# A second attention with doubled query and key columns, whole transposes, alternating value products and head norms from one square

## The chip, the cores and the metric

The kernel runs on one core of a Trainium2 chip. The metric is the device time of one execution in microseconds (us), the median of the runs shown. A profiled execution gives the span of its instructions and a trace. In its rows PE is TensorE (matrix products and transposes), PEld its weight loads, DVE is VectorE, ACT is ScalarE, POOL is GpSimd and SP the engine that issues most loads.

## The reference, cut to what matters

Two transformer blocks of two layers each follow each other on 256 tokens of width 1024. The change lies in the second layer of the second block (an attention that also reads 256 context tokens) and in two helpers that earlier layers use too.

```python
qkv = h_lat @ w_qkv
q = rmsnorm(qkv[..., :Q_DIM].reshape(B, S, N_Q_HEADS, HEAD_DIM), q_g)      # 16 heads of 64
k = rmsnorm(qkv[..., Q_DIM:Q_DIM + KV_DIM].reshape(B, S, N_KV_HEADS, HEAD_DIM), k_g)   # 4 heads
q = apply_rope(q, cos, sin)
k = apply_rope(k, cos, sin)
kv_c = h_ctx @ w_qkv[:, Q_DIM:]
k_all = jnp.concatenate([k_c, k], axis=1)     # 256 context + 256 own tokens
v_all = jnp.concatenate([v_c, v], axis=1)
s = jnp.einsum('bqhgd,bkhd->bhgqk', q_blk, k_all)
p = jax.nn.softmax(s, axis=-1)
o = jnp.einsum('bhgqk,bkhd->bqhgd', p, v_all)
```

## The kernel before, in words

All weights come from DRAM as a fixed list of pieces. Each piece lands in a buffer (`raw`, or a lent `page`), ScalarE rounds it to a high part `H` (L309) and VectorE forms the low part `L`, the rest (L310); a product takes three matrix products, high by high, low by high and high by low (`mm3`, L149 to L151). Between the weights stand pieces of the modulation matrices, which VectorE multiplies by a scalar and accumulates (L353). When eight of those are summed, `ada_piece` reduces them over the 128 rows, in most cases with transposes and eight ScalarE activations that sum along the row (L364) and whose elementwise output, `adump`, nobody reads.

The order on each engine is decided by a scheduler when the program is built, from the order of the code and priorities; an engine then takes its instructions strictly in that order. Tiles come from rotating pools: PSUM has three banks `mm`, four `acc` and one `tr`; 512-column work tiles are called `q1` to `q4`, two buffers each.

Block 1 (two layers) norms its query and key heads with `head_rstd`: one ScalarE square of 64 columns with a sum for each head (L617), then a power on GpSimd. `head_rope` rotates: two products with tables of cosines and sines (L635, L636), one difference and one sum (L639, L640).

`attention2` is the second attention. Four projections give keys and values of 256 context and 256 own tokens (`kpost`), two more give the queries of eight heads each (`qpost`). Scores need query and key with the 64 head columns on the partitions, twice: the query's high part in one half of the 128 rows and its low part in the other, the key's high part in both halves, so that one product gives both. `twice` does that from rows of 64 columns a head: for each of four heads one transpose into rows 0 to 63 (L1519) and one product with the identity into rows 64 to 127 (L1520, two instructions on the engine). `kH` and `kL` are the key's two parts; `kL` holds two of the four key heads in rows 0 to 63 and two in rows 64 to 127. Work that `later` defers runs some projection parts later.

Then a loop over 16 heads, in which step i does `S(i)`, the scores and their softmax, `T(i-1)`, the transposes of the probabilities, and `O(i-2)`, the product with the values:

- `S`: for each of two token tiles a product with `kH` on 128 rows (L1576) and one with `kL` on 64 rows (L1577), VectorE's maximum (L1579), ScalarE's exponent with its sum (L1583), VectorE's reciprocal and scaling (L1584, L1585).
- `T`: eight 128x128 transposes (L1594) and two ScalarE copies to `pT` (L1597).
- `O`: four products of a 128x64 value tile (L1608, eight instructions on the engine); even heads write rows 0 to 63 and odd heads rows 64 to 127 of one PSUM bank, which is read after the odd head (L1612, L1613).

Behind it come the output projection and the expert layer.

Of the kernel before, what the change touches and what calls it, by code (L numbers as in the profile page):

```python
# [24 lines left out]
P = 128  # L25
# [58 lines left out]
class Kern:  # L84
# [256 lines left out]
    def ada_piece(s, raw, m, j, q):  # L341
# [12 lines left out]
        if q == 7:  # L354
            for v in vecs:
                if (m, j) not in ((0, 0), (0, 1)) and (m < 3 or j == 1):
                    u = s.st([P, 8], tag="acol8", bufs=4)
                    for h in range(2):
# [3 lines left out]
                        for i in range(4):  # L362
                            o = s.st([P, P], tag="adump", bufs=1)
                            nc.scalar.activation(o, t[:, i * P:(i + 1) * P], AF.Copy, accum_out=u[:, 4 * h + i:4 * h + i + 1])  # L364
# [26 lines left out]
    def far_row(s, col, new=None):  # L391
        """as row, through DRAM"""
# [200 lines left out]
    def kt(H, Lo, t):  # L593
        """the k tiles of token tile t"""
# [16 lines left out]
    def head_rstd(s, src, nh):  # L611
        """src [P, nh*64] -> 1 / rms of each head"""
        nc = s.nc
        ss = s.st([P, 8], tag="hss", bufs=4)
        for h in range(nh):
            o = s.st([P, P], tag="adump", bufs=1)
            nc.scalar.activation(o[:, 0:64], src[:, h * 64:(h + 1) * 64], AF.Square, scale=0.125, accum_out=ss[:, h:h + 1])  # L617
# [11 lines left out]
    def head_rope(s, qn, nh, CG, SG, w, dst, psum=False):  # L629
# [7 lines left out]
        hv = lambda t: t[:, 0:n].rearrange("p (a b w) -> p a b w", b=2, w=w)  # L637
        c, sn, d = hv(qc), hv(qs), hv(dst)
# [3 lines left out]
    def block1(s, l):  # L642
# [80 lines left out]
        # output projections of the two attentions, gated  # L723
# [33 lines left out]
        # mlp  # L757
# [93 lines left out]
    def proj(s, ps, X, key, kk, n, post=None, first=True, last=True, tmajor=False, late=False):  # L851
        """n half pieces of kk k-tiles against the token tiles; late: the low parts last"""
# [127 lines left out]
    def lat_rows(s):  # L980
        """the rows that the pool layer needs for x, made ahead"""
# [45 lines left out]
    def pre0(s, X):  # L1027
        """pool mixer, then the router's logits and the rows that the experts gather"""
# [26 lines left out]
    def slots0(s, t0, before=(), slot0=None):  # L1055
        """where the expert inputs and weights of two token tiles go in the slots"""
# [39 lines left out]
    def ctx_steps(s):  # L1096
        """the pool layer's work on the context, in steps, each after the modulation vectors that it needs"""
# [37 lines left out]
    def ctx_step(s, last=False):  # L1135
        """the next step if its vectors are there; all that is left if last"""
# [57 lines left out]
    def ranks(s, M16, n, before=()):  # L1194
        """M16 [P, 2, n] 0/1 -> [P, 3, n]: how many came before, and the counts"""
# [17 lines left out]
    def dense_rest(s, l, fl, hD, ovg, Xs, rows, bank, hT, mo, wt):  # L1213
        """tokens that found no slot: every expert over all tokens, weighed by ovg"""
# [89 lines left out]
    def router(s, Ac, Sc):  # L1304
        """the router's weights with the norm's gain in them, and its bias with the shift"""
# [182 lines left out]
    def attention2(s):  # L1488
# [111 lines left out]
        def O(h):  # L1600
            b = (h % 2) * 64
            if h % 2 == 0:
                ops[h // 2] = s.mm()
# [257 lines left out]
```

## Time and profile before

| | |
|---|---|
| device time, median of 3 runs | 1524.44 us (1520.88 to 1526.36) |
| span of the profiled execution | 1517.5 us |
| median less that span | 6.9 us |
| TensorE busy | 1386.3 us, 91% of the span |
| VectorE busy | 1175.7 us, 77% |
| ScalarE busy | 936.0 us, 62% |
| mean granted clock of TensorE | 0.951 |

Which of the runs was profiled isn't marked, so its own time is taken as the span and the 6.9 us by which the median lies above it. A share over the whole span mixes stages with different limits; the rows below are cut by stage. TensorE's products are pipelined, so that one product's duration is longer than the distance to the start of the next; paces are read from starts. A granted clock of 1.00 is 2.4 GHz and 0.50 is 1.2 GHz.

### The profile page before, as it was taken

The numbers are of one execution on the slowest core, as the hardware profiler recorded it, in microseconds if no ns is written. First come the engines' busy times: TensorE is split into PE (matmuls) and PEld (weight loads), VectorE is DVE, ScalarE is ACT, GpSimd is POOL, SyncE is SP. The second block draws the span as 40 slices with busy tenths as digits, with TensorE's granted clock in tenths as the row PEclk, the third lists the DMA queues.
The fourth block names the chain that finished last, engine by engine and source line by source line (L and its number), as shares of the span: only waits on it lengthen the run. The fifth ranks groups of instructions, "written<-read, shape, count | busy, mean of one in ns | idle before, by whom it ended". The sixth has DMA issues, their size and how long they took to land. (4 is left out here: it accounts for less than half of the span.)

```text
span 1517.5 us, 21071 instructions
## 1 busy us (share of the span) xinstructions
PE 1386.3 (91%) x7103; PEld 1071.7 (71%) x7103; DVE 1175.7 (77%) x1711; ACT 936.0 (62%) x2014; POOL 194.9 (13%) x183
## 2 busy tenths in 40 slices
PE   3899998999999999979999986998889999989898
PEld 2666776989977666768898875776556645776565
DVE  6885688776769887989998785897886645488787
ACT  2686745666567857566756443886754546458674
POOL 0221021000003110220000222222111210020000
PEclk9998999999999999989999996999999959989999
DMA  9673776897966665877889876999973540139982
GB/s 357 226 269 118 239 266 225 313 320 261 337 208 209 199 189 167 295 256 271 283 293 332 274 263 223 272 291 303 327 268 127 191 155 1 42 128 340 363 267 83
DMA packets 193339, 362.25 MB, mean 239 GB/s; under 512 B 20046, under 2 KB 91190, under 8 KB 193216
## 3 DMA queue, kind: packets, MB, share of 16 engines
q1 hardware_dynamic: 189024, 351.26, 68.7%
q0 software_dynamic: 3360, 7.91, 2.3%
q10 hardware_dynamic: 832, 1.57, 0.3%
q8 instruction: 60, 0.98, 0.3%
q14 instruction: 63, 0.52, 0.1%
HBM read 351.70 MB, written 12.88 MB: 240 GB/s over the span
## 5 line engine op out<-in xcount | busy, mean ns | idle before, releaser
L309 ACT CAST H<-raw 128x1024 fp32r<-128x1024 f32 x331 | 346.1, 1050 | 219.1 <-PE acc L151 91.6
L310 DVE TENSOR_TENSOR L<-raw,H 128x1024 fp32r<-128x1024 f32 x331 | 409.6, 1246 | 81.1 <-ACT H L309 77.1
L353 DVE SCALAR_TENSOR_TENSOR page<-raw,sc,page 128x1024 f32<-128x1024 f32 x218 | 283.1, 1308 | 28.2 <-DMA raw<-in_w_ada_dram 14.6
L149 PE MATMUL mm<-H,page 128*128 128x512 f32 (+1 forms) x416 | 167.9, 405 | 19.1 <-ACT page L581 10.9
L150 PE MATMUL mm<-L,page 128*128 128x512 f32 (+1 forms) x416 | 164.5, 396 | 1.0 <-DVE L L310 1.0
L151 PE MATMUL mm<-H,page 128*128 128x512 f32 (+1 forms) x416 | 164.0, 395 | 1.4 <-DVE page L582 1.3
L310 DVE TENSOR_TENSOR L<-page,H 128x1024 fp32r<-128x1024 f32 x104 | 125.4, 1222 | 30.1 <-ACT H L309 27.4
L150 PE MATMUL acc<-L,page 128*128 128x512 f32 x352 | 139.2, 395 | 0.0
L149 PE MATMUL acc<-H,page 128*128 128x512 f32 x352 | 139.0, 395 | 0.0
L151 PE MATMUL acc<-H,page 128*128 128x512 f32 x352 | 138.9, 395 | 0.0
L309 ACT CAST H<-page 128x1024 fp32r<-128x1024 f32 x104 | 108.5, 1051 | 41.2 <-PE mm L151 23.2
L798 PE MATMUL mm<-page,L 128*128 128x256 f32 x448 | 127.6, 285 | 0.0
L795 PE MATMUL mm<-page,H 128*128 128x256 f32 x448 | 127.5, 285 | 0.0
L797 PE MATMUL mm<-page,H 128*128 128x256 f32 x448 | 127.2, 284 | 0.0
L149 PE MATMUL mm<-H,gH 128*96 128x512 f32 x256 | 105.8, 413 | 9.6 <-PEq L1217 5.9
L149 PEld LDWEIGHTS mm<-H,page 128*128 128x128 f32 x416 | 80.1, 193 | 42.9 <-ACT page L581 13.2
L151 PE MATMUL mm<-H,gL 128*96 128x512 f32 x256 | 103.9, 406 | 1.6 <-DVE gL L1391 1.6
L150 PE MATMUL mm<-L,gH 128*96 128x512 f32 x256 | 103.2, 403 | 0.0
L151 PEld LDWEIGHTS mm<-H,page 128*128 128x128 f32 x416 | 79.9, 192 | 20.3 <-DVE page L582 3.9
L150 PEld LDWEIGHTS mm<-L,page 128*128 128x128 f32 x416 | 80.4, 193 | 18.1 <-issue 2.7
L795 PEld LDWEIGHTS mm<-page,H 128*128 128x128 f32 x448 | 85.8, 192 | 0.6
L797 PEld LDWEIGHTS mm<-page,H 128*128 128x128 f32 x448 | 85.8, 192 | 0.5
(381 smaller groups left out, 2693.4 us busy)
## 6 DMA issues: line engine op xcount, KB each, us to landing
raw<-in_w_mod_dram SPq DMA_DIRECT2D x94, 512.0 KB
raw<-in_w_ada_dram SPq DMA_DIRECT2D x92, 512.0 KB
raw<-in_w_in_dram SPq DMA_DIRECT2D x68, 512.0 KB
raw<-in_w_up_dram SPq DMA_DIRECT2D x61, 512.0 KB
raw<-in_w_down_dram SPq DMA_DIRECT2D x61, 512.0 KB
page<-in_moe_wd_dram SPq DMA_DIRECT2D x36, 512.0 KB
raw<-in_moe_wg_dram SPq DMA_DIRECT2D x64, 256.0 KB
raw<-in_moe_wu_dram SPq DMA_DIRECT2D x64, 256.0 KB
```

The lines of the kernel that those rows point to most:

```text
L149: mm(ps, sH, wH, start=start, stop=False)
L150: mm(ps, sH, wL, start=False, stop=False)
L151: mm(ps, sL, wH, start=False, stop=stop)
L309: s.nc.scalar.copy(H, src)
L310: s.nc.vector.tensor_sub(Lo, src, H.bitcast(F32))
L353: nc.vector.scalar_tensor_tensor(a, raw, c, a, ALU.mult, ALU.add)
L795: nc.tensor.matmul(o, a, H[q // 2][:, 2 * (q % 2) + k], start=q == 0 and k == 0 and f % 2 == 0, stop=False, skip_group_check=True)
L797: nc.tensor.matmul(o, a, Lo[q // 2][:, 2 * (q % 2) + k], start=False, stop=False, skip_group_check=True)
L798: nc.tensor.matmul(o, b, H[q // 2][:, 2 * (q % 2) + k], start=False, stop=q == 3 and k == 1 and f % 2 == 1, skip_group_check=True)
```

## The change

Four things change in the second attention. Query and key rows are written with each head's 64 columns doubled (`head_rope` with `twice=True`, and the context key's product with its gain), so that a whole 128x128 transpose gives both halves; `twice` is now four transposes. The query's low part always lies in rows 64 to 127, and `kL` holds all four key heads on all 128 rows, so that the second score product takes 128 rows too (it then also adds low by low). `O` runs once for two heads and alternates between them product by product, and it is written ahead of `T`. In `head_rstd`, which block 1 uses as well, one square over all heads and one VectorE sum take the place of a square with a sum for each head. In `ada_piece` the unread output goes back to the PSUM columns that it came from. Hunks that only remove comments are left out here.

```diff
@@ ada_piece
-                            o = s.st([P, P], tag="adump", bufs=1)
-                            nc.scalar.activation(o, t[:, i * P:(i + 1) * P], AF.Copy, accum_out=u[:, 4 * h + i:4 * h + i + 1])
+                            o = t[:, i * P:(i + 1) * P]
+                            nc.scalar.activation(o, o, AF.Copy, accum_out=u[:, 4 * h + i:4 * h + i + 1])
@@ head_rstd
-        for h in range(nh):
-            o = s.st([P, P], tag="adump", bufs=1)
-            nc.scalar.activation(o[:, 0:64], src[:, h * 64:(h + 1) * 64], AF.Square, scale=0.125, accum_out=ss[:, h:h + 1])
+        o = s.st([P, 512], tag="q3", bufs=2)[:, 0:nh * 64]
+        nc.scalar.activation(o, src, AF.Square, scale=0.125)
+        nc.vector.tensor_reduce(ss[:, 0:nh], o.rearrange("p (h d) -> p h d", d=64), AX.X, ALU.add)
@@ head_rope
+        if twice:
+            hv = lambda t, u=1: t[:, 0:n * u].rearrange("p (h u r b w) -> p h u r b w", h=nh, u=u, b=2, w=w)
+            c, sn = hv(qc), hv(qs)
+            dst = dst if isinstance(dst, list) else [dst]
+            m = nh // len(dst)
+            for i, d in enumerate(dst):
+                d, g = d[:, 0:2 * n // len(dst)].rearrange("p (h u r b w) -> p h u r b w", h=m, u=2, b=2, w=w), slice(i * m, (i + 1) * m)
+                for u in range(2):
+                    nc.vector.tensor_sub(d[:, :, u, :, 0], c[:, g, 0, :, 0], sn[:, g, 0, :, 1])
+                    nc.vector.tensor_add(d[:, :, u, :, 1], c[:, g, 0, :, 1], sn[:, g, 0, :, 0])
+            return
@@ attention2
-        kL = s.bt([P, 2, 512], F32R, tag="kL")
+        kL = s.bt([P, 4, 512], F32R, tag="kL")
...
-                src = rows[:, c0 + 64 * i:c0 + 64 * i + 64]
-                nc.tensor.transpose(ps[0:64, i * P:(i + 1) * P], src, s.ident)
-                nc.tensor.matmul(ps[64:128, i * P:(i + 1) * P], src, s.ident, start=True, stop=True)
+                nc.tensor.transpose(ps[:, i * P:(i + 1) * P], rows[:, c0 + P * i:c0 + P * i + P], s.ident)
...
-            for b in range(2):
-                r, g = slice(64 * b, 64 * b + 64), slice(2 * b, 2 * b + 2)
-                nc.vector.tensor_sub(kL[r, :, tok], ps[r, g], kH[r, g, tok].bitcast(F32))
-
-        def q_T(rows, c0, dst, b):
+            nc.vector.tensor_sub(kL[:, :, tok], ps, kH[:, :, tok].bitcast(F32))
+
+        def q_T(rows, c0, dst):
...
-            r = slice(64 - 64 * b, 128 - 64 * b)
+            r = slice(64, 128)
...
-                s.head_rope(kn, 4, CG[:, 1, i - 2], SG[:, 1, i - 2], 16, dst)
+                s.head_rope(kn, 4, CG[:, 1, i - 2], SG[:, 1, i - 2], 16, dst, twice=True)
...
-                dst = s.st([P, 512], tag="q4", bufs=2)
-                s.head_rope(pq[t], 8, CG[:, 0, t], SG[:, 0, t], 16, dst, True)
+                dst = [s.st([P, 512], tag=tag, bufs=2) for tag in ("q4", "q2")]
+                s.head_rope(pq[t], 8, CG[:, 0, t], SG[:, 0, t], 16, dst, True, twice=True)
...
-                nc.tensor.matmul(ps, q[r, t * P:(t + 1) * P], kL[r, h // 4 % 2], start=False, stop=True)
+                nc.tensor.matmul(ps, q[:, t * P:(t + 1) * P], kL[:, h // 4], start=False, stop=True)
...
         def O(h):
-            b = (h % 2) * 64
             if h % 2 == 0:
-                ops[h // 2] = s.mm()
-            ps = ops[h // 2]
-            p = pts.pop(h)
+                return
+            ps = s.mm()
+            p = [pts.pop(h - 1), pts.pop(h)]
             c = (h // 4) * 64
             for i in range(4):
-                nc.tensor.matmul(ps[b:b + 64, 0:256], v[:, i, c:c + 64], p[:, i], start=i == 0, stop=i == 3)
+                for b in range(2):
+                    nc.tensor.matmul(ps[64 * b:64 * b + 64, 0:256], v[:, i, c:c + 64], p[b][:, i], start=i == 0, stop=i == 3)
...
+            if i >= 2:
+                O(i - 2)
             if 1 <= i < 17:
                 T(i - 1)
-            if i >= 2:
-                O(i - 2)
```

The first place is TensorE's order where the projections end (`mm`, fed from the weights `H` and `L`) and the second attention's first scores (`kH`, `kL` by the query pages) are followed by the transposes of the last query tiles (`q` to `acc`; `cst` holds the identity). Before, where the pair of rows of L1519 and L1520 comes sixteen times in all:

```order
L151 MATMUL mm_14886<-H_14925,page_14342 128x512
L1576 MATMUL acc_15091<-kH_14459,page_14707 128x512
L1577 MATMUL acc_15091<-kL_14460,page_14707 128x512
L1576 MATMUL acc_15102<-kH_14459,page_14707 128x512
L1577 MATMUL acc_15102<-kL_14460,page_14707 128x512
L369 MATMUL tr_14980<-ones,page_14783 128x1 x8
L1519 MATMUL acc_15113<-cst,q_3384_15046 64x128
L1520 MATMUL acc_15113<-cst,q_3384_15046 64x128
```

And now:

```order
L1583 MATMUL acc_14663<-kH_14107,page_14324 128x512
L1584 MATMUL acc_14663<-kL_14108,page_14324 128x512
L1583 MATMUL acc_14674<-kH_14107,page_14324 128x512
L1584 MATMUL acc_14674<-kL_14108,page_14324 128x512
L1530 MATMUL acc_14685<-cst,q_3073_14617 128x128 x4
L1530 MATMUL acc_14692<-cst,q_3074_14618 128x128 x4
L1530 MATMUL acc_14699<-cst,q_3082_14645 128x128 x4
L1530 MATMUL acc_14706<-cst,q_3083_14646 128x128 x4
L1583 MATMUL acc_14713<-kH_14107,page_14324 128x512
```

Four rows of four whole transposes stand where thirty-two rows stood, the scores of the next head follow at once, and the eight sums of one column (L369) have moved into the loop.

The second place is TensorE's order in the loop: transposes of probabilities (`q` to `mm`) and products of values `v` with transposed probabilities `pT`. Before, for heads 2 and 3:

```order
L1594 MATMUL mm_15302<-cst,q_3450_15250 128x128 x4
L1576 MATMUL acc_15313<-kH_14459,page_14708 128x512
L1577 MATMUL acc_15313<-kL_14460,page_14708 128x512
L1608 MATMUL mm_15308<-pT_3451_15254,v_14461 64x256 x4
L1576 MATMUL acc_15324<-kH_14459,page_14708 128x512
L1577 MATMUL acc_15324<-kL_14460,page_14708 128x512
L1594 MATMUL mm_15336<-cst,q_3457_15280 128x128 x4
L1594 MATMUL mm_15342<-cst,q_3461_15291 128x128 x4
L1608 MATMUL mm_15308<-pT_3462_15295,v_14461 64x256 x4
```

And now:

```order
L1616 MATMUL mm_14886<-pT_3135_14816,v_14109 64x256
L1583 MATMUL acc_14910<-kH_14107,page_14325 128x512
L1584 MATMUL acc_14910<-kL_14108,page_14325 128x512
L1583 MATMUL acc_14921<-kH_14107,page_14325 128x512
L1601 MATMUL mm_14898<-cst,q_3141_14836 128x128 x3
L1616 MATMUL mm_14886<-pT_3146_14851,v_14109 64x256
L1616 MATMUL mm_14886<-pT_3135_14816,v_14109 64x256
L1616 MATMUL mm_14886<-pT_3146_14851,v_14109 64x256
L1616 MATMUL mm_14886<-pT_3135_14816,v_14109 64x256
```

The two heads' value products, which stood as two separate rows of four, now alternate (three more such rows follow), with the first of them alone ahead of some scores.

The third place is VectorE's order behind the last query projection: the rotation of the two token tiles, the first head's maxima `mx` and, now, the sums `hss` of the norms. Before:

```order
L635 TENSOR_TENSOR q_3385_15047<-mm_14885,CG_14453 128x512
L636 TENSOR_TENSOR q_3386_15048<-mm_14885,SG_14454 128x512
L1580 TENSOR_TENSOR mx_15094<-mx_15094,qsc_14462 128x1
L1579 TENSOR_REDUCE mx_15105<-acc_15102 128x1
L639 TENSOR_TENSOR q_3384_15046<-q_3385_15047,q_3386_15048 128x16x16
L640 TENSOR_TENSOR q_3384_15046<-q_3385_15047,q_3386_15048 128x16x16
L635 TENSOR_TENSOR q_3400_15081<-mm_14886,CG_14453 128x512
```

And now, where the two last rows come four times, twice for each of the two tiles `q`:

```order
L617 TENSOR_REDUCE hss_14609<-q_3071_14610 128x8
L635 TENSOR_TENSOR q_3075_14619<-mm_14485,CG_14101 128x512
L636 TENSOR_TENSOR q_3076_14620<-mm_14485,SG_14102 128x512
L617 TENSOR_REDUCE hss_14637<-q_3080_14638 128x8
L646 TENSOR_TENSOR q_3073_14617<-q_3075_14619,q_3076_14620 128x4x2x16
L647 TENSOR_TENSOR q_3073_14617<-q_3075_14619,q_3076_14620 128x4x2x16
```

The first head's maxima, which stood between the two tiles' rotations, now stand behind the second tile's products.

## Rows read from the trace of the kernel before

**Rows 1.** The head of the page: the span of the profiled execution.

```profile
span 1517.5 us, 21071 instructions
```

**Rows 2.** Busy time by stage (columns: stretch, length, engines busy, granted clock, DMA).

```profile
1157.60:1210.20 52.60, 51.72 (x236) 35.35 (x234) 36.31 (x53) 26.41 (x81) 10.60 (x12) 0.98 0.42 141
1210.20:1231.10 20.90, 19.19 (x70) 9.14 (x68) 10.86 (x23) 9.53 (x35) 5.19 (x6) 0.59 0.33 101
1231.10:1248.00 16.90, 16.90 (x40) 8.77 (x39) 9.63 (x30) 8.13 (x19) 0.00 (x0) 0.50 0.68 223
1248.00:1311.10 63.10, 63.10 (x290) 36.51 (x288) 32.05 (x102) 36.52 (x83) 0.00 (x0) 1.00 0.05 16
1311.10:1517.50 206.40, 186.75 (x855) 137.22 (x854) 161.36 (x210) 129.36 (x167) 11.44 (x11) 0.94 0.66 225
40.00:140.00 100.00, 89.59 (x425) 65.73 (x424) 78.55 (x176) 71.47 (x236) 24.73 (x24) 0.95 0.66 217
440.00:560.00 120.00, 107.92 (x515) 81.69 (x513) 101.05 (x163) 89.28 (x284) 27.46 (x28) 0.96 0.62 193
```

**Rows 3.** Groups by line, 1157.6 to 1311.1 (busy us, mean ns, idle before).

```profile
L1520 PE MATMUL acc<-cst,q 128*64 128x128 f32 x96 | 25.3, 353 | 0.0
L1583 ACT ACTIVATE q<-acc,mx,qsc 128x512 f32<-128x512 f32 x32 | 24.9, 785 | 3.2 <-DVE mx L1580 3.0
L1579 DVE TENSOR_REDUCE mx<-acc 128x1 f32<-128x512 f32 x32 | 21.9, 688 | 27.6 <-PE acc L1577 27.3
L1597 ACT COPY pT<-mm 128x512 f32<-128x512 f32 x32 | 18.3, 586 | 24.2 <-PE mm L1594 24.0
L617 ACT ACTIVATE adump<-mm 128x64 f32<-128x64 f32 x32 | 7.2, 224 | 1.8 <-PE mm L151 0.4 <-POOL q L635 0.4
L1583 ACT ACTIVATION_READ_ACCUMULATOR q<-acc,mx,qsc 128x1 f32 x32 | 6.5, 204 | 0.0
L353 DVE SCALAR_TENSOR_TENSOR page<-raw,sc,page 128x1024 f32<-128x1024 f32 x5 | 6.4, 1281 | 0.1
```

**Rows 4.** TensorE in order of time, query transposes (start, length).

```profile
1201.92 0.27 PE L1519 MATMUL acc<-cst,q 128*64 128x128 f32 x1
...
1206.63 0.50 PE L149 MATMUL mm<-H,page 128*128 128x512 f32 x1
...
1215.44 0.39 PE L1519 MATMUL acc<-cst,q 128*64 128x128 f32 x1 [1.71 <-DVE q L640]
...
1231.15 1.12 PE L1594 MATMUL mm<-cst,q 128*128 128x128 f32 x4
```

**Rows 5.** TensorE in order of time: the loop and the next projection.

```profile
1260.15 0.50 PE L1576 MATMUL acc<-kH,page 128*128 128x512 f32 x1
1260.57 0.49 PE L1577 MATMUL acc<-kL,page 64*128 64x512 f32 x1
1260.99 0.66 PE L1594 MATMUL mm<-cst,q 128*128 128x128 f32 x4
1261.41 0.48 PE L1576 MATMUL acc<-kH,page 128*128 128x512 f32 x1
...
1272.22 1.94 PE L1608 MATMUL mm<-pT,v 128*64 128x256 f32 x8
...
1308.29 2.86 PE L1608 MATMUL mm<-pT,v 128*64 128x256 f32 x16
...
1313.04 0.39 PE L149 MATMUL acc<-H,page 128*128 128x512 f32 x1
1313.27 0.39 PE L150 MATMUL acc<-L,page 128*128 128x512 f32 x1
```

**Rows 6.** VectorE in order of time: rotations of a key and a query tile.

```profile
1186.27 0.28 DVE L639 TENSOR_TENSOR q<-q,q 128x128 f32<-128x128 f32 x1
1186.47 0.28 DVE L640 TENSOR_TENSOR q<-q,q 128x128 f32<-128x128 f32 x1
...
1212.67 0.69 DVE L635 TENSOR_TENSOR q<-mm,CG 128x512 f32<-128x512 f32 x1 [0.95 <-ACT adump L617]
```

More of the change, by code (lines that the diff above doesn't have):

```diff
@@ L627, in head_norm, with head_rope @@
         return qn
-    def head_rope(s, qn, nh, CG, SG, w, dst, psum=False):
+    def head_rope(s, qn, nh, CG, SG, w, dst, psum=False, twice=False):
         nc = s.nc
@@ L1542, in kpost @@
             if i < 2:
-                nc.vector.tensor_mul(dst[:, 0:256].rearrange("p (h d) -> p h d", d=64),
-                                     kn[:, 0:256].rearrange("p (h d) -> p h d", d=64),
-                                     s.gain2[:, 1:2].to_broadcast([P, 4, 64]))
+                nc.vector.tensor_mul(dst.rearrange("p (h u d) -> p h u d", h=4, u=2),
+                                     kn[:, 0:256].rearrange("p (h d) -> p h d", d=64)[:, :, None, :].to_broadcast([P, 4, 2, 64]),
+                                     s.gain2[:, 1:2, None, :].to_broadcast([P, 4, 2, 64]))
             else:
-                s.head_rope(kn, 4, CG[:, 1, i - 2], SG[:, 1, i - 2], 16, dst)
+                s.head_rope(kn, 4, CG[:, 1, i - 2], SG[:, 1, i - 2], 16, dst, twice=True)
             s.later(lambda: k_T(dst, slice(i * P, (i + 1) * P)), 3)
@@ L1560, in qpost @@
                 nc.gpsimd.tensor_scalar(qsc[:, t, 8 * c:8 * c + 8], r, 0.125, 0.0, ALU.mult, ALU.add)
-                dst = s.st([P, 512], tag="q4", bufs=2)
-                s.head_rope(pq[t], 8, CG[:, 0, t], SG[:, 0, t], 16, dst, True)
+                dst = [s.st([P, 512], tag=tag, bufs=2) for tag in ("q4", "q2")]
+                s.head_rope(pq[t], 8, CG[:, 0, t], SG[:, 0, t], 16, dst, True, twice=True)
                 for b in range(2):
-                    s.later(lambda b=b: q_T(dst, 256 * b, qT[c][b][:, :, t * P:(t + 1) * P], c), 3 + b)
+                    s.later(lambda b=b: q_T(dst[b], 0, qT[c][b][:, :, t * P:(t + 1) * P]), 3 + b)
             s.proj(pq, X, ("qkv", c), 2, 4, qpost)
@@ L1568, in attention2 @@
         o = [s.hl4() for _ in range(2)]
-        sms, pts, ops = {}, {}, {}
+        sms, pts = {}, {}
         def S(h):
-            r = slice(64 * (h // 8), 64 * (h // 8) + 64)
             q = qT[h // 8][h // 4 % 2][:, h % 4]
@@ L1600, in O @@
         def O(h):
-            b = (h % 2) * 64
             if h % 2 == 0:
-                ops[h // 2] = s.mm()
-            ps = ops[h // 2]
-            p = pts.pop(h)
+                return
+            ps = s.mm()
+            p = [pts.pop(h - 1), pts.pop(h)]
             c = (h // 4) * 64
             for i in range(4):
-                nc.tensor.matmul(ps[b:b + 64, 0:256], v[:, i, c:c + 64], p[:, i], start=i == 0, stop=i == 3)
-            if h % 2:
-                oH, oL = o[h // 8]
-                i = h // 2 % 4
-                nc.scalar.copy(oH[:, i], ps[:, 0:256])
-                nc.vector.tensor_sub(oL[:, i], ps[:, 0:256], oH[:, i].bitcast(F32))
+                for b in range(2):
+                    nc.tensor.matmul(ps[64 * b:64 * b + 64, 0:256], v[:, i, c:c + 64], p[b][:, i], start=i == 0, stop=i == 3)
+            oH, oL = o[h // 8]
+            i = h // 2 % 4
+            nc.scalar.copy(oH[:, i], ps[:, 0:256])
+            nc.vector.tensor_sub(oL[:, i], ps[:, 0:256], oH[:, i].bitcast(F32))
         for i in range(18):
```

## The prediction

> **What bounds the kernel now.** I read the stage table first, which cuts the second attention into its parts and sets block 1 beside it; then the groups of instructions by line, for counts and means; then TensorE's order of time, for the pace at which one instruction follows another; last two places of VectorE's order.
>
> The profiled execution spans 1517.5 us [rows 1]. The second attention's part from the first key transpose to the last value product lasts 153.5 us of it, and TensorE is the engine that is never free there: busy 51.7 of 52.6, 19.2 of 20.9, 16.9 of 16.9 and 63.1 of 63.1 us, while VectorE and ScalarE are busy half to 70% of the time and DMA nearly rests in the last part (share 0.05) [rows 2]. I call these parts A (key and query projections up to 1210.2), B (up to 1231.1: the last query transposes), C1 and C2 (the loop over 16 heads). The granted clock is 0.98 in A, falls to 0.59 in B and 0.50 in C1, and is 1.00 in C2 [rows 2]. So time that TensorE saves in these stages is saved in the kernel, until another engine takes over. Nothing behind them gives it back: DMA stands idle in C2 because every buffer is full, and the 206.4 us from 1311.1 on [rows 2] begin with the weights that lie there and start their next loads when the loop ends, so that stage moves forward as a whole.
>
> Much of TensorE's busy time is not streaming. A group of `twice` (one transpose into rows 0 to 63 and one product with the identity, two instructions, into rows 64 to 127) is issued 48 times (96 instructions on the second line [rows 3]). Eight groups run from 1201.92 to 1206.63, 0.59 us each at full clock; sixteen, with one small transpose among them, from 1215.44 to 1231.15, 0.98 us each at half clock [rows 4]. Four 128x128 transposes that are followed by a score product take 1260.99 to 1261.41, 0.42 us together [rows 5]. A score pair takes 0.42 for the product on 128 rows and 0.42 for the one on 64 rows (1260.15, 1260.57, 1260.99), where two 512-column products of one shape follow each other in 0.23 (1313.04, 1313.27) [rows 5]. Eight value instructions of one head take 1.94 us (1272.22) [rows 5].
>
> **The change, part by part.**
>
> A. Each `twice` becomes four whole transposes. Eight of the twelve calls lie in A: 8 x (4 x 0.59 - 0.42) = 15.5 us less for TensorE, 51.7 to 36.2. VectorE gets more. The head norms add four reductions of 256 columns and two of 512; at 0.69 for 512 [rows 3] and half of it for 256 that is 2.8 us. The doubled writing turns two operations of 256 columns into eight of 128 for each query tile, and two of 128 into four for each key tile with rotation. One of 128 follows the next in 0.20 us (1186.27, 1186.47), the larger two in some 0.33 each (a bound: their sum against 0.69 for 512), so +0.9 for a query and +0.4 for a key tile: 2.6 us for two of each. The two context key tiles multiply 512 columns instead of 256, +0.35 each by the same halving; k's low part is one subtraction of 128 rows by 512 columns instead of two of 256, which I take as even. Sum about +6: VectorE goes from 36.3 [rows 2] to 42 us, less three accumulations of 1.28 us each [rows 3], which the new order puts behind the first scores: 38. So VectorE, not TensorE's 36.2, becomes the floor of A. With nothing overlapping perfectly A may end between 37 (TensorE alone) and 45 (VectorE's wait for each square added); I take 40, **12.5 us saved**.
>
> B. Now the second tile's rotation stands behind sixteen small squares on ScalarE; VectorE waited 0.95 us for them at 1212.67 [rows 6], each square is 0.22 us and has a reading of its sum behind it [rows 3]. One square of 512 columns costs about 0.59 (the copy of the same shape [rows 3]), and the reduction behind it 0.69. From the end of the projections: square done before it, reduction to 0.2, two products of at most 0.69 [rows 6] to 1.5, the second reduction to 2.1, four small operations to 2.9, the first four transposes; then 0.8, 1.3 for the second tile's products, 0.6 for a maximum that the order puts between, and twice 0.8: the last transposes start near 7.2 and end near 8.0, at half clock. B is 20.9 now [rows 2], so **13 us saved**. Queued behind VectorE's longer rotation are the first head's maxima; what waits for them is ScalarE's exponent, not TensorE, which has the scores of heads 1 and 2 next. The query tiles now need two tags (`q4`, `q2`); their readers, the transposes, are done one projection later, so I charge no wait.
>
> C. The low product takes 128 rows, so no shape changes inside a score pair: 0.84 to 2 x 0.23, 0.38 less for 30 pairs, 11 us. The values of two heads alternate between rows 0 to 63 and 64 to 127 of the output. The trace shows this overlap once: at 1308.29 the last two heads' sixteen instructions follow each other and take 2.86 us, not 2 x 1.94 = 3.88; half of them overlap, so alternating all should save twice the 1.02, 1.84 to about 2.1 us a pair. In the new order the first product of a pair is mostly issued alone and the rest after some scores, which costs one more change of shape, about 0.35 (0.42 + 0.42 against 0.46 gives 0.19 a change, two of them). So eight pairs cost 8 x 2.45 = 20 instead of 31, 11 us less (bounds: nothing, if the overlap needs a queue that runs ahead, and 14). TensorE's work in C is then 60 x 0.23 + 128 x 0.105 + 20 + 2 (the next projection's first products) = 49 us at full clock. VectorE has 9.6 + 32.1 [rows 2] and gets the three accumulations and two weight differences of as many columns moved here, all at 1.28, 48; ScalarE has 8.1 + 36.5 = 45 [rows 2] (by means 2 x (0.785 + 0.204 + 0.586) = 3.15 a head [rows 3], 50). Three engines of equal load in chains of seven steps a head don't run at their floor: I take 62 us with some 4 us of half clock in it, against 80.0 now, **18 us saved**; the ends are 52 and 78.
>
> The skill speaks against the alternation: the Trainium skill, "TensorEngine Tiling (Array Packing)", section PSUM Bottleneck, says that tiling speeds up TensorE but not the emptying of PSUM, which may become the limit. By that rule the alternation's 11 us would go to ScalarE's and VectorE's waits and C would end near 73. The trace agrees that the margin is thin: those engines come out 1 to 4 us below TensorE's new need [rows 2, 3].
>
> Block 1 uses the same head norms. For each layer 52 squares go from ScalarE and VectorE gets six reductions of 512 columns and two small ones, 4.6 us. TensorE idles 10.4 of 100 and 12.1 of 120 us there, VectorE is busy 79% and 84% [rows 2]. Bounds: 9 us lost, if all of it lands on the path twice, and 8 gained, if a third of that idle time was waiting for squares; I take zero. The modulation sums write their dump back into PSUM: 192 instructions at perhaps 50 ns more or less (an estimate, a quarter of the 0.22 us row [rows 3]) on an engine that TensorE rarely waits for; zero, with 5 us to either side.
>
> Sum: 12.5 + 13 + 18 = 43.5 us. The median shown, 1524.4, is 6.9 above the span of this execution; the same lies around the new one: 1517.5 - 43.5 + 6.9 = 1481.
>
> **Rivals.**
> - *The alternation doesn't overlap.* For it: each product is two instructions, and in the one place seen the overlap starts only when the second head's work reaches the engine. Against it: it does start there. C gains 11 less on TensorE and about 8 in time: 1489.
> - *ScalarE and VectorE bind.* C ends at 73 and A at 44: 8.5 + 13 + 7 = 28.5 saved, 1496. For it the near equal sums, against it their idle time now.
> - *The clock stays low through the loop.* For it: B and C1 ran at 0.59 and 0.50 while TensorE was busy all the time, mostly with transposes and changes of shape [rows 2]. Against it: C2 ran at 1.00 with 8 transposes a head. TensorE's 49 us become 92: C loses 12, 13.5 saved in all: 1511. The Trainium skill, "TensorE: Matmul & The Clock Gate", Part 4, says that transposes don't count as busy for the clock in the same way; the trace agrees in B and not in C2 [rows 2].
> - *Slower: the low clock begins in A.* If the shorter transposes let it fall from the key projections on, A's 36.2 us of TensorE become 72, 20 more than now, and C loses 12 while B gains 12: 1544. It turns the sign once about 43 us of full-clock TensorE work run at half; against it stands 0.98 in A with longer pauses than will be left.
>
> **Chances.** Forecast 0.60, its own range 1468 to 1490; no overlap 0.10; ScalarE and VectorE 0.14; low clock in the loop 0.06; slower 0.03; more than forecast, below 1468, with block 1's gain added, 0.07. The range 1466 to 1503 leaves out the two clock cases, half of the last one, and some tails. A change under 0.3% (4.6 us), about what a measurement of this kernel can tell from none, would need a partial low clock: 0.03. Slower 0.04, with a little for block 1's order; faster 0.93.
>
> **What would show it.** Right: four transposes of `twice` in 0.4 to 0.6 us; the first scores of head 1 some 8 us after those of head 0; score products 0.23 apart; sixteen value instructions of a pair in about 2 us; A, B and C near 40, 8 and 62; the stretch behind the loop still about 206. Wrong: TensorE in the loop waiting for ScalarE's copies or VectorE's scaling in most heads; a granted clock of 0.50 for more than some 20 us of the loop; block 1 longer by over 5 us a layer.

## The result and the profile after

| | before | after |
|---|---|---|
| device time, median of 4 runs each on one chip | 1522.66 us (1517.29 to 1526.36) | 1467.66 us (1466.21 to 1473.28) |
| ratio | | 0.967, 95% interval 0.964 to 0.970 |
| span of the profiled execution | 1517.5 us [rows 1] | 1464.4 us, in a run of 1466.67 |

The change makes the kernel 3.3% faster, 50 us (46 to 54 by the interval). The two medians above differ by 55; in three later sets of 11 to 17 runs the kernel before had medians of 1518.12 to 1520.18, which goes with the 50. 1481 was forecast, with a range of 1466 to 1503. Cut as in [rows 2], with the parts A, B, the loop (C1 and C2 together), the stretch behind it and the two windows of block 1, the profile after reads (the third and the fifth row cut the time around B and the loop once more, into the stretch of half clock and the rest of the loop; columns: length, then the busy time of TensorE, its weight loads, VectorE, ScalarE and GpSimd, then the granted clock and DMA):

```profile
1146.30:1185.90 39.60, 37.73 (x170) 30.42 (x171) 34.34 (x64) 20.60 (x31) 11.39 (x12) 0.95 0.46 146
1185.90:1197.10 11.20, 4.06 (x22) 2.89 (x20) 11.04 (x30) 6.28 (x10) 4.41 (x6) 0.74 0.28 94
1191.30:1201.60 10.30, 6.00 (x23) 4.76 (x23) 10.11 (x24) 5.59 (x10) 0.55 (x2) 0.50 0.16 51
1197.10:1257.30 60.20, 58.28 (x345) 38.24 (x343) 48.25 (x143) 43.71 (x103) 0.00 (x0) 0.96 0.38 123
1201.60:1257.30 55.70, 53.99 (x331) 34.96 (x329) 43.81 (x135) 42.26 (x100) 0.00 (x0) 1.00 0.39 124
1257.30:1464.40 207.10, 186.92 (x856) 137.00 (x855) 161.66 (x211) 129.32 (x167) 11.40 (x11) 0.94 0.66 224
40.00:140.00 100.00, 94.20 (x452) 70.03 (x450) 84.06 (x193) 65.56 (x153) 26.55 (x24) 0.97 0.69 228
440.00:560.00 120.00, 112.45 (x556) 82.70 (x554) 103.66 (x187) 84.98 (x212) 25.39 (x26) 0.99 0.60 189
```

| us saved, by the two profiled executions | forecast | measured |
|---|---|---|
| ahead of A (block 1 and the rest) | 0 | 1157.6 - 1146.3 = 11.3 |
| A | 12.5 | 52.6 - 39.6 = 13.0 |
| B | 13 | 20.9 - 11.2 = 9.7 |
| the loop | 18 | 80.0 - 60.2 = 19.8 |
| behind the loop | 0 | 206.4 - 207.1 = -0.7 |
| sum | 43.5 | 53.1 |

The second attention came out within 1 us of its forecast, 42.5 of 43.5. (Cut alike, at the first scores of head 1, B saved 10.5 and the loop 18.9.) The miss lies ahead of it, where TensorE's idle time in the two windows of block 1 fell from 10.4 and 12.1 us [rows 2] to 5.8 and 7.5.

B is where the changed kernel still waits. TensorE in order of time, with the idle time ahead of an instruction and what ended it in brackets:

```profile
1186.62 0.40 PE L1584 MATMUL acc<-kL,page 128*128 128x512 f32 x1
1189.89 0.63 PE L1530 MATMUL acc<-cst,q 128*128 128x128 f32 x4 [2.87 <-DVE q L647]
1190.70 0.63 PE L1530 MATMUL acc<-cst,q 128*128 128x128 f32 x4 [0.18 <-DVE q L647]
1195.41 2.03 PE L1530 MATMUL acc<-cst,q 128*128 128x128 f32 x8 [4.09 <-DVE page L1542]
1197.10 0.78 PE L1583 MATMUL acc<-kH,page 128*128 128x512 f32 x1
```

The second tile's transposes wait not for the rotation but for L1542, which forms the low part of the first tile out of a PSUM bank and is that bank's last reader; VectorE comes to it late:

```profile
1193.28 0.28 DVE L647 TENSOR_TENSOR q<-q,q 128x128 f32<-128x128 f32 x1
1193.48 0.28 DVE L646 TENSOR_TENSOR q<-q,q 128x128 f32<-128x128 f32 x1
1193.68 0.28 DVE L647 TENSOR_TENSOR q<-q,q 128x128 f32<-128x128 f32 x1
1193.89 0.14 DVE L1587 TENSOR_TENSOR mx<-mx,qsc 128x1 f32<-128x1 f32 x1
1193.96 0.68 DVE L1586 TENSOR_REDUCE mx<-acc 128x1 f32<-128x512 f32 x1
1194.66 0.69 DVE L1542 TENSOR_TENSOR page<-acc,page 64x512 fp32r<-64x512 f32 x1
```

And the loop, one step of it in TensorE's order:

```profile
1241.52 0.65 PE L1616 MATMUL mm<-pT,v 128*64 128x256 f32 x2
1242.10 0.50 PE L1583 MATMUL acc<-kH,page 128*128 128x512 f32 x1
1242.43 0.40 PE L1584 MATMUL acc<-kL,page 128*128 128x512 f32 x1
1242.66 0.40 PE L1583 MATMUL acc<-kH,page 128*128 128x512 f32 x1
1242.90 0.39 PE L1584 MATMUL acc<-kL,page 128*128 128x512 f32 x1
1243.13 0.27 PE L1601 MATMUL mm<-cst,q 128*128 128x128 f32 x1
1243.33 1.94 PE L1616 MATMUL mm<-pT,v 128*64 128x256 f32 x14
1245.20 0.99 PE L1601 MATMUL mm<-cst,q 128*128 128x128 f32 x7
```

In this step score products follow each other in 0.23 us, and in 0.33 behind a tile of another shape. A pair's sixteen value instructions take 0.58 and 1.87, together 2.45 us, where one head took 1.94 before [rows 5].

### The profile page after: what moved, and what is told of

The parts are those of the page before. It is cut to its first block, busy times and chain, and to the rows that moved or that the text cites. A ratio compares the mean times of both kernels' runs of the same rounds, so it can differ in the third digit from the quotient of the medians.

```text
span 1464.4 us, 20599 instructions
## 1 busy us (share of the span) xinstructions
PE 1330.7 (91%) x7007; PEld 1050.7 (72%) x7007; DVE 1187.1 (81%) x1759; ACT 907.4 (62%) x1734; POOL 193.2 (13%) x183
## 5 line engine op out<-in xcount | busy, mean ns | idle before, releaser
L149 PE MATMUL mm<-H,page 128*128 128x512 f32 (+1 forms) x416 | 167.4, 404 | 14.8 <-ACT page L581 10.5
L151 PEld LDWEIGHTS mm<-H,page 128*128 128x128 f32 x416 | 80.3, 193 | 19.8 <-DVE page L582 4.3
```

What stands on the lines that cost most here:

```text
L149: mm(ps, sH, wH, start=start, stop=False)
L151: mm(ps, sL, wH, start=False, stop=stop)
```

## The experiments

Each was timed in turns with the kernel before; the ratios are to it, with 95% intervals. Differences between rows go by the ratios, since the runs come from several sets.

| | time, us | ratio | start of A | A | B | loop |
|---|---|---|---|---|---|---|
| the kernel before | 1522.66 | 1 | 1157.6 | 52.6 | 21.7 | 79.1 |
| the changed kernel | 1467.66 | 0.9672 (0.9643 to 0.9701) | 1146.3 | 39.6 | 11.2 | 60.2 |
| norms alone | 1507.27 | 0.9922 (0.9897 to 0.9947) | 1146.1 | 54.3 | 18.8 | 84.8 |
| dump alone | 1510.32 | 0.9954 (0.9933 to 0.9976) | 1148.7 | 51.9 | 21.7 | 79.2 |
| own buffer for squares | 1504.24 | 0.9891 (0.9863 to 0.9919) | 1147.7 | 55.0 | 18.4 | 79.8 |
| squares reversed | 1516.77 | 0.9988 (0.9968 to 1.0008) | 1147.7 | 52.0 | 21.7 | 79.0 |
| norms, dump and low part | 1493.27 | 0.9823 (0.9787 to 0.9858) | 1147.0 | 54.3 | 17.9 | 68.5 |
| changed, values in sequence | 1469.01 | 0.9667 (0.9639 to 0.9694) | 1150.2 | 39.1 | 11.2 | 63.1 |
| changed, low part on 64 rows | 1480.94 | 0.9749 (0.9723 to 0.9775) | 1147.7 | 42.0 | 11.5 | 75.5 |
| changed, old transposes | 1486.15 | 0.9774 (0.9746 to 0.9801) | 1149.1 | 55.6 | 16.2 | 58.6 |
| changed, values as before | 1473.38 | 0.9688 (0.9657 to 0.9719) | 1150.0 | 39.0 | 11.2 | 68.4 |
| changed, late transposes | 1463.89 | 0.9643 (0.9615 to 0.9671) | 1144.6 | 40.2 | 70.8 with the loop | |
| changed, copies by ScalarE | 1463.81 | 0.9643 (0.9608 to 0.9678) | 1139.9 | 40.1 | 9.3 | 61.8 |
| changed, both of these | 1463.80 | 0.9636 (0.9602 to 0.9670) | 1142.0 | 40.5 | 69.5 with the loop | |

Here B ends with head 1's first scores. The start of A and the lengths are those of one profiled execution each. Kernels with the same code ahead of A started it between 1139.9 and 1150.2, so a start is good to some 5 us only; the lengths repeat within 1 us (A and B of the two kernels whose values alone differ).

**Where the 11 us ahead of the second attention come from.** The norms alone:

```diff
-        for h in range(nh):
-            o = s.st([P, P], tag="adump", bufs=1)
-            nc.scalar.activation(o[:, 0:64], src[:, h * 64:(h + 1) * 64], AF.Square, scale=0.125, accum_out=ss[:, h:h + 1])
+        o = s.st([P, 512], tag="q3", bufs=2)[:, 0:nh * 64]
+        nc.scalar.activation(o, src, AF.Square, scale=0.125)
+        nc.vector.tensor_reduce(ss[:, 0:nh], o.rearrange("p (h d) -> p h d", d=64), AX.X, ALU.add)
```

> The kernel before with one part of the change alone: head norms by one ScalarE square and one VectorE sum. In the changed kernel's trace the stretch ahead of the second attention's first key transpose is 11.3 us shorter (1146.3 against 1157.6), where the prediction took zero. Theory (the norms give it: the chain square, sum, power, rotation is shorter in block 1 and TensorE waits behind it): the stretch ends 8 to 13 us earlier here too, in two steps of about 5 and 8 us, one in each of block 1's attentions; with 2 to 3 us from the second attention's last queries the time is 10 to 15 us below before. Rival (the modulation sums without a dump give it, the norms are neutral as predicted): 0 to 3 us below before, all of it behind 1157.

The dump alone (the change's hunk in `ada_piece`, nothing else):

> The kernel before with another part alone: the modulation sums write their unread output back into PSUM. Theory (the norms give block 1's 11.3 us): no change, within 3 us, and no step in block 1; the mean of the summing ScalarE activation may move by some 50 ns. Rival (the dump in SBUF, one buffer shared with the head squares, held ScalarE up): 8 to 11 us faster.

Both came out faster, by about 12 and 7 us, and both with a start of A some 10 us earlier; the kernels that have both, the changed one and the one with norms, dump and low part, start A no earlier. Each side was half right. (The norms also shortened B by 2.9 us, and their loop stood longer at half clock.) So the squares got a buffer of their own, their number unchanged:

```diff
-            o = s.st([P, P], tag="adump", bufs=1)
+            o = s.st([P, 512], tag="q3", bufs=2)
             nc.scalar.activation(o[:, 0:64], src[:, h * 64:(h + 1) * 64], AF.Square, scale=0.125, accum_out=ss[:, h:h + 1])
```

> The kernel before with one edit: the head squares write their unread output to a work tile of two buffers (the one that the changed head norm uses) instead of the single buffer that the modulation sums write too; number and kind of instructions stay. Norms alone moved the second attention's start from 1157.6 to 1146.1, the dump alone to 1148.7, both together to 1146.3, so they are not additive. Theory (what both took away is the one buffer that the two users share; it ties the norms behind the modulation sums when the order is made): the start comes at 1146 to 1150 here too and the time is 6 to 11 us below before. Rival (each gives its own gain, by fewer instructions or a cheaper output): start unchanged within 3 us.

That alone gave some 16 us (ratio 0.9891), more than expected. It is no less than the norms' 12, so no gain of the single square beyond the buffer is shown. The control leaves the buffer shared and only writes the heads in reverse:

```diff
-        for h in range(nh):
+        for h in reversed(range(nh)):
```

> A control: the kernel before with the head squares written in the reverse order of heads; the shared buffer and the number of instructions stay. Giving the squares a buffer of their own brought the second attention's start from 1157.6 to 1147.7. Theory (the shared buffer makes the poor order in block 1): start within 3 us of 1157.6, time within 0.4% of before. Rival (the scheduler's order is a draw, and the kernel before had a bad one; whatever changes it gives 8 to 11 us): start near 1147, 8 to 14 us below before.

Its time is that of before (0.9988, 1 included). Its profiled execution, the fastest of its twelve (1509.62), started A at 1147.7, as the rival would have it, so one start decides nothing here; the times speak for the shared buffer, with one other order of the squares as the only control. The waits agree: those of GpSimd's power on the head squares and of TensorE, between 80 and 160 us and between 40 and 150 (total, times, longest), first with the squares reversed, then with their own buffer:

```profile
POOL rstd L155 <- ACT adump L617: 25.4, 3, 20.3
...
PE acc L666 <- DVE den L924: 2.3, 1, 2.3
```

```profile
POOL rstd L155 <- ACT q L617: 17.9, 3, 10.3
```

The 20.3 and TensorE's 2.3 are in the kernel before to the digit, and gone with the own buffer. In block 1's second layer (440 to 570) GpSimd's power waits 58.6 and 61.5 us for the head squares or their sums in the two kernels with the shared buffer, and 36 to 39 in the twelve without it.

But a start of A also hangs on the clock. The time up to A in the kernel before, with the squares reversed, with their own buffer, and in the changed kernel:

```profile
0.00:1157.60 1157.60, 1048.62 (x5621) 844.75 (x5621) 925.46 (x1295) 726.03 (x1630) 167.69 (x154) 0.96 0.78 260
0.00:1147.70 1147.70, 1039.76 (x5621) 839.78 (x5621) 924.81 (x1294) 726.35 (x1631) 169.30 (x154) 0.97 0.79 262
0.00:1147.70 1147.70, 1044.68 (x5620) 843.79 (x5620) 923.05 (x1296) 721.13 (x1631) 169.27 (x154) 0.96 0.79 263
0.00:1146.30 1146.30, 1043.70 (x5621) 842.18 (x5621) 931.84 (x1314) 707.53 (x1425) 166.02 (x154) 0.97 0.79 263
```

TensorE has the same number of instructions ahead of A, to one record. With the squares reversed it is idle for 107.9 us, hardly less than the 109.0 of the kernel before; the earlier start is 8.9 us of busy time, at a higher granted clock. With their own buffer it is idle for 103.0 us, in the changed kernel 102.6, and in the other kernels without the shared buffer 101 to 107. So of the 11.3 us ahead of A some 6.4 are waiting time, and the other 4.9 are busy time of the same instructions, a difference between two single executions. The times agree: 50 us less the second attention's 42.5 leave 7 (3 to 12 by the interval). Why the own buffer alone gave 16 us (12 to 21) in time stays open: its profiled execution, the slowest of its five (1509.75), shows 5 to 6 us less waiting.

The order in which the squares stand on ScalarE is another one; by which step of the scheduler one buffer brings that about was not tried.

**The low part on 64 rows again**, in the changed kernel (the core of the edit):

```diff
-            r = slice(64, 128)
+            r = slice(64 - 64 * b, 128 - 64 * b)
...
-                nc.tensor.matmul(ps, q[:, t * P:(t + 1) * P], kL[:, h // 4], start=False, stop=True)
+                nc.tensor.matmul(ps, q[r, t * P:(t + 1) * P], kL[r, h // 4 % 2], start=False, stop=True)
```

> The changed kernel with k's low part on 64 rows again (the score's second product takes 64 rows, q's low part lies in the other half as before). Theory (a change of shape costs twice 0.19 us in each score pair): products 0.42 apart instead of 0.23, 32 pairs x 0.38 = 12 us, less what already stands beside other shapes now (in about half the pairs something stands between the two products): 8 to 12 us slower than the changed kernel, 1476 to 1480. Rival (the loop's pace comes from ScalarE and VectorE by now): under 4 us.

12 us slower by the ratios, at the upper end of the forecast, but not by shape alone. The loop in two stretches, and a score pair at full clock:

```profile
1201.20:1224.50 23.30, 23.30 (x68) 13.42 (x67) 12.67 (x35) 7.83 (x18) 0.00 (x0) 0.50 0.15 46
1224.50:1276.70 52.20, 51.59 (x277) 29.96 (x277) 35.81 (x108) 36.37 (x85) 0.00 (x0) 1.00 0.37 122
```

```profile
1240.03 0.51 PE L1586 MATMUL acc<-kH,page 128*128 128x512 f32 x1
1240.46 0.49 PE L1587 MATMUL acc<-kL,page 64*128 64x512 f32 x1
1240.88 0.50 PE L1586 MATMUL acc<-kH,page 128*128 128x512 f32 x1
```

The pair takes 0.43 and 0.42 again. But the loop spends 23.3 us at half clock (1.2 GHz) with TensorE busy throughout, against 4.5 in the changed kernel (1197.1 to 1201.6). Half of the difference, 9.4 us, is, as an estimate, the clock's share of the 15.3 that the loop grew; the shape itself is left with 6. From the other side, on the kernel before with norms and dump (the core of the edit):

```diff
-            r = slice(64 - 64 * b, 128 - 64 * b)
+            r = slice(64, 128)
...
-                nc.tensor.matmul(ps, q[r, t * P:(t + 1) * P], kL[r, h // 4 % 2], start=False, stop=True)
+                nc.tensor.matmul(ps, q[:, t * P:(t + 1) * P], kL[:, h // 4], start=False, stop=True)
```

> The kernel before with the head norms' one square, the dump in PSUM (both make the room) and k's low part on all 128 rows; transposes of query and key and the value products stay as before. Undoing the low part alone in the changed kernel made the loop 15.4 us longer (75.5 against 60.1) with the granted clock low for 31 us instead of 10. Theory (the 64-row products cost 0.38 a pair and also keep the clock down; the transposes of 64 columns don't): the loop falls from 79 to 85 us to 62 to 69, the clock is low for 10 to 15 us, part A and B stay near 53 and 19; with the 11 ahead of A some 30 us below before, 1488. Rival (the clock's low stretch belongs to the long queue of half transposes): the loop falls by 11 only, to 70 to 73, with over 25 us of low clock.

The loop is 68.5, in the range of the theory; against the norms alone (which lack the dump) it falls by 16.3 and the time by 15 us. Against the kernel before the time is 27 us less, where 30 was expected. The low stretch shrinks from 37.5 to 17.0 us, more than the theory's 15 and less than the rival's 25:

```profile
1203.70:1241.20 37.50, 37.48 (x109) 20.28 (x110) 18.13 (x46) 12.69 (x26) 1.58 (x2) 0.50 0.06 18
```

```profile
1205.30:1222.30 17.00, 17.00 (x53) 8.45 (x52) 8.65 (x19) 5.41 (x10) 1.96 (x2) 0.50 0.00 0
```

(norms alone, then with the low part).

**The old transposes**, in the changed kernel:

```diff
-                nc.tensor.transpose(ps[:, i * P:(i + 1) * P], rows[:, c0 + P * i:c0 + P * i + P], s.ident)
+                src = rows[:, c0 + P * i:c0 + P * i + 64]
+                nc.tensor.transpose(ps[0:64, i * P:(i + 1) * P], src, s.ident)
+                nc.tensor.matmul(ps[64:128, i * P:(i + 1) * P], src, s.ident, start=True, stop=True)
```

> The changed kernel with the old form of the query and key transposes (a transpose of 64 columns into rows 0 to 63 and a product with the identity into rows 64 to 127, for each head), all else as changed. Theory (the prediction's sizes): part A grows by 8 x (4 x 0.59 - 0.42) = 15.5 us of TensorE less its present 2 us of pauses, 13; part B, where TensorE now waits for VectorE in 7 of 11.2 us, by 4 to 9; together 17 to 22 us slower than the changed kernel, 1485 to 1490. Rival (these groups also keep the granted clock at half for longer, as in the kernel before until the loop's 17th us): the loop grows too, by up to 15, and the sum is 25 to 37. Rival (VectorE sets A by now, 34.3 busy of 39.6): A grows by under 8.

15.5 us slower by the ratios and 18.5 by the medians, where 17 to 22 was expected: A grew by 16, B by 5, the loop not at all, and the clock was low for as long as in the changed kernel:

```profile
1214.50:1224.70 10.20, 10.20 (x34) 6.06 (x34) 6.41 (x12) 3.32 (x7) 0.00 (x0) 0.50 0.17 51
```

Both rivals fall. With the last two runs, the long low clock of the kernel before goes with the 64-row score products and not with the half transposes. Why it lasted 17 us with whole low parts in the old kernel, and 10 here, stays open.

**The value products.** In sequence, at the same places:

```diff
-            for i in range(4):
-                for b in range(2):
+            for b in range(2):
+                for i in range(4):
```

> The changed kernel, but the two heads' value products one head after the other (four products into rows 0 to 63, then four into rows 64 to 127), at the same places in the order. Measured with alternation: a pair is 0.57 for the first product and 1.87 for the other seven, 2.45 us. Theory (the alternation itself overlaps the two halves): without it a pair takes near 2 x 1.94 = 3.9, the loop grows by 8 x 1.4 = 11 us, 1467 to 1479. Rival (it is enough that two heads stand next to each other; the last two heads of the kernel before took 2.86): a pair near 2.9, 3 to 4 us. Rival (ScalarE and VectorE set the pace of the loop): no change, TensorE idle instead.

No change in time that can be told; the loop is 2.9 longer. TensorE, six of the eight pairs:

```profile
1217.74 1.94 PE L1616 MATMUL mm<-pT,v 128*64 128x256 f32 x8
1219.61 0.33 PE L1601 MATMUL mm<-cst,q 128*128 128x128 f32 x1
1220.00 1.94 PE L1616 MATMUL mm<-pT,v 128*64 128x256 f32 x8
...
1225.65 3.21 PE L1616 MATMUL mm<-pT,v 128*64 128x256 f32 x16
1232.86 3.56 PE L1616 MATMUL mm<-pT,v 128*64 128x256 f32 x16
1240.11 3.31 PE L1616 MATMUL mm<-pT,v 128*64 128x256 f32 x16
...
1254.63 2.99 PE L1616 MATMUL mm<-pT,v 128*64 128x256 f32 x16
1260.85 2.86 PE L1616 MATMUL mm<-pT,v 128*64 128x256 f32 x16
```

Seven pairs stand next to each other and take 2.86 to 3.56 us; in the one at 1217.74 a transpose stands between the heads, and each takes 1.94. So two heads next to each other overlap by themselves, as in the first rival, but less than when they alternate: from start to start, without pauses, the eight pairs take 25.6 us of TensorE here and 19.7 in the changed kernel. Then one head at a time and behind the transposes, as in the kernel before:

```diff
...
-            for i in range(4):
-                for b in range(2):
-                    nc.tensor.matmul(ps[64 * b:64 * b + 64, 0:256], v[:, i, c:c + 64], p[b][:, i], start=i == 0, stop=i == 3)
+            for i in range(4):
+                nc.tensor.matmul(ps[b:b + 64, 0:256], v[:, i, c:c + 64], p[:, i], start=i == 0, stop=i == 3)
...
-            if i >= 2:
-                O(i - 2)
             if 1 <= i < 17:
                 T(i - 1)
+            if i >= 2:
+                O(i - 2)
```

> The changed kernel with the value products as before: one head at a time, behind the next head's transposes. Products of two heads that alternate took 2.45 us a pair; in sequence but next to each other 2.9 to 3.6 and no difference in time that could be told. Theory (what counts is that the two heads stand next to each other): the order now puts other tiles between most of them, near 3.9 a pair, 8 x 1.4 = 11 us slower than the changed kernel in TensorE's work and some 8 in time, 1476. Rival (ScalarE and VectorE hide it, as the small effect of the last run would have it): under 3.

The loop grew by 8.2, with most heads alone at 1.94 (two of the eight pairs happen to stand next to each other, at 2.86):

```profile
1242.32 1.94 PE L1615 MATMUL mm<-pT,v 128*64 128x256 f32 x8
1244.78 1.94 PE L1615 MATMUL mm<-pT,v 128*64 128x256 f32 x8
```

The products take 28.3 us here. The time grew by 2 (by the ratio) to 6 us (by the medians), between the rival's 3 and the theory's 8; the intervals overlap, so the loop's length is the firmer witness. Of its 8.2 us 5.3 go with the heads standing next to each other (and ahead of the transposes) and 2.9 with alternating; of TensorE's own work it is 2.7 and 5.9.

**Part B.** The last query transposes one by one in the loop's steps:

```diff
-            if i == 1:
-                s.drain()
+            if i in (2, 3, 4, 5) and s.fq:
+                heapq.heappop(s.fq)[2]()
```

> The changed kernel with the last four groups of query transposes not ahead of head 1's scores but one each in the loop's steps 2 to 5 (heads 0 to 7 don't read them). In the changed kernel part B is 11.2 us, 3.0 of waiting for VectorE's rotation and 4.1 for its subtractions, which free the PSUM banks; the granted clock then is 0.54 to 0.59 for 12 us. Theory (TensorE's order makes the wait): it goes on with scores and part of the wait and of the low clock disappears, 3 to 7 us faster than the changed kernel, 1461 to 1465. Rival (VectorE, busy 11.0 of the 11.2, sets the pace of B whatever TensorE's order is): within 2 us of the changed kernel, the wait now in front of the first probabilities' transposes.

The second copy of the query columns by ScalarE:

```diff
...
-                for u in range(2):
+                for u in range(2 - psum):
...
+                if psum:
+                    nc.scalar.copy(e[:, :, 1], e[:, :, 0])
```

> The changed kernel with the second copy of the query's 64 columns written by ScalarE (one copy of 256 columns for each page) instead of four more VectorE operations of 128 columns. Moving TensorE's transposes out of part B gained nothing there (B and the loop 70.8 against 71.3), so VectorE should set it. Theory: VectorE's work in B falls by 8 x 0.2 = 1.6 us, ScalarE, idle for 5 of 11 us there, hides its copies: 1 to 2 us faster than the changed kernel. Rival (the copy stands behind the rotation in the same chain and adds its 0.4 us and a wait for each tile): even or 1 us slower.

And both:

> The changed kernel with both: the last query transposes in the loop's steps 2 to 5, and the second copy of the query columns by ScalarE. Theory (VectorE sets the stretch from the first scores to the first probabilities' transposes, and the transposes' wait for the copies is off the path): 2 to 5 us faster than the changed kernel, about 1463. Rival: no better than either alone.

All three are some 4 us below the changed kernel by the medians, with ratios whose intervals overlap its own. In the place that they change, little happened: B and the loop together take 70.8, 71.1 and 69.5 against 71.4, and part of the rest is an earlier start of A, which they don't touch. With both, TensorE waits once, and longer:

```profile
1184.13 0.40 PE L1587 MATMUL acc<-kL,page 128*128 128x512 f32 x1
1191.18 1.11 PE L1533 MATMUL acc<-cst,q 128*128 128x128 f32 x4 [6.65 <-ACT q L1593]
```

That fits VectorE as the pace of B, whose queue holds both rotations ahead of the first heads' maxima; an order with the maxima first was not tried. None of the three is shown to beat the changed kernel.

## Why the prediction was right, and where it was off

The sign, the range and the second attention's sum were right. The total, 1467.66, lies just below the forecast's own range (1468 to 1490), in the case that got 0.07: block 1's gain on top. That the second attention's sum came within 1 us is partly luck: B gave 3.3 less than forecast, A and the loop 2.3 more.

- **Block 1 and the dump.** The step that failed is "I take zero". The bounds for the norms, 9 us lost and 8 gained, were drawn for fewer instructions; by the experiments the gain came from another side, the output buffer that both users shared, and either edit brought it. Norms alone measured 12 us in time, dump alone 7. In the changed kernel it is some 6 to 7 of the 11.3 us that the two traces show; the rest is the busy time of two single executions.
- **A**: 39.6 for 40; putting the half transposes back lengthened it by 16.0, and 15.5 had been worked out for TensorE. But the bound named was wrong: TensorE's 37.7 stayed above VectorE's 34.3, which had been put at 38.
- **B**: 11.2 for 8. VectorE's rotations ended 8.0 us behind the first scores (near 1194) where 7.2 had been worked out. The term left out is the PSUM bank: the transposes of the second tile were to start then, and waited until 1195.41 for the first tile's subtraction.
- **The loop**: 60.2 for 62, with errors that cancel. VectorE was busy for 48.3 us of it and ScalarE for 43.7, much as worked out (48 and 45). But TensorE's need was put at 49 us and it was busy for 58.3, and the chains between three equal engines cost little: at full clock TensorE is busy 54.0 of 55.7 us. The mis-sized term is the score products, 60 at 0.23 or 13.8 us: 59 take 18.8 from start to start, because other instructions stand between many of them and the first ran at half clock; the sixteen one-column sums (L369), 1.7 us, had no term. The value products came as worked out, 2.45 us a pair and 19.7 in all, though part of that overlap needs no alternation. The low part was put at 11 us; put back, it cost 15, by the estimate above 6 of shape and 9 of clock. ScalarE and VectorE did not become the limit. By the rule that the prediction weighed, the Trainium skill, "TensorEngine Tiling (Array Packing)", section PSUM Bottleneck, which it gives for a fourfold speedup, the loop would have ended near 73; here the emptying of PSUM did not become the limit.
- **The clock**: 4 us of it low were allowed in the loop, 4.5 came. Neither low-clock rival happened; in A it stood at 0.95. (The first one's 92 us for TensorE's 49 at half clock is a slip: twice 49 is 98, which makes that rival 6 us dearer.) With the old transposes the low stretch was as long, 10.2 us against 10.3. The rule cited there, the Trainium skill, "TensorE: Matmul & The Clock Gate", Part 4, that transposes don't count as busy for the clock in the same way, is not tested by that: the old form has as many transposes, and products beside them.
- **The base**: 6.9 us were put around the span. But every run whose own span is listed lies 2.0 to 2.6 us above it (the profiled one 2.3), so most of the 6.9 was the distance of that execution from the median shown. The new median lies 3.3 above the new span; the other 3.6 are part of the 13.3 us by which 1481 missed.

## What to carry to other kernels

A buffer for an output that nobody reads, shared by two users of one engine, can tie them to each other: give each its own, or write into a tile that is dead anyway, before counting instructions. Value products for two halves of the output rows overlapped here when they stood next to each other (2.86 to 3.56 us a pair instead of twice 1.94) and more when they alternated (2.45), so first bring the heads together in the order, and then ask whether to interleave. When a helper is called elsewhere, give its call sites a sum of their own; the stretch ahead of the second attention was most of this prediction's error. And before an earlier start of a stage is credited to an edit, compare the engine's busy and idle time up to it: here a control with the old waits started 10 us earlier all the same.

## What was unexpected of the hardware

The granted clock fell to 0.50 behind the projections in every one of these kernels, but came back at different times: after 7 to 10 us in the changed kernel and its variants with whole low parts, the old transposes among them, after 17 with whole low parts in the old kernel, 31 to 37 wherever the second score product had 64 rows, although TensorE was then busy without a pause (23.3 of 23.3 us). By these runs the shape of the products costs more than its own 0.2 us each: of the 15 us that it cost here, an estimated 9 were the clock.
